# Gathers paced by the phase of the routing, experts looked up by two ranks, weighted one-hots on two engines

## The chip, the core and the metric

One core of a Trainium2 chip runs the whole program. The metric is the device time of one execution in microseconds, over three runs: median 3159.07 us (3156.07 to 3160.61). Engines are named as in the profile: PE (matrix products), DVE (vector), ACT (activations), POOL (GpSimd, which issues the gathers), SP (which issues most plain DMAs).

## The reference, cut to what matters

The program is two transformer blocks over 512 tokens of width 1024, in float32. The change is inside the feed-forward part of the first, a product-key mixture of 16384 experts with eight heads and 16 experts a head and token:

```python
def peer_ffn(h, wq, sub_keys, u, v):
    tok = h.reshape(-1, PEER_BLOCK, D)               # blocks of 128 tokens
    def block(t):
        q = (t @ wq).reshape(PEER_BLOCK, PEER_HEADS, 2, PEER_DQ // 2)
        s = jnp.einsum('tpcd,pckd->tpck', q, sub_keys)
        s1, i1 = lax.top_k(s[:, :, 0], PEER_TOPK)    # 16 of 128 first keys
        s2, i2 = lax.top_k(s[:, :, 1], PEER_TOPK)    # 16 of 128 second keys
        cand = (s1[..., :, None] + s2[..., None, :]).reshape(PEER_BLOCK, PEER_HEADS, 256)
        cidx = (i1[..., :, None] * PEER_NKEYS + i2[..., None, :]).reshape(PEER_BLOCK, PEER_HEADS, 256)
        top, pos = lax.top_k(cand, PEER_TOPK)
        idx = jnp.take_along_axis(cidx, pos, axis=-1)
        g = jax.nn.softmax(top, axis=-1)
        a = jax.nn.gelu(jnp.einsum('tpkd,td->tpk', u[idx], t), approximate=False)
        return jnp.einsum('tpk,tpkd->td', g * a, v[idx])
    return lax.map(block, tok)
```

## The kernel before, in words

The expert part does the same thing in two ways. For block 0 of the tokens it fetches the rows of U and V of each chosen expert. For blocks 1 to 3 it computes all experts densely: expert number e = 128 a + b, and a *hidden layer* (`hidden`, called 128 times, "an expert" in what follows is one such call) multiplies 128 rows of U with the 384 tokens of the three blocks and applies Gelu; a gate matrix W, zero where nothing was chosen, weights the result; the *products* multiply it with 128 rows of V.

**The routing** (`route`, L1199) goes through five phases t. In phase t below 4 `topk` (L1236) finds the experts of block t, on DVE: 16 scans of 128 scores (`top16`, L1228: two `max`, two `max_index` and one `match_replace` each), then 50 candidate sums and their 50 expert numbers, then a scan of the candidates of each head, which gives the place of each of 16 winners among the 50. The number is looked up by comparing the place with 0 to 49 (`eq`, L1271), multiplying by the candidates' numbers (L1273) and summing (L1274). Exp and a sum make the gates. In phases 2 to 4 `spread` (L1296) turns block t - 1 into the gate matrix: for each group of four tokens DVE compares 0 to 127 with the first half of the expert numbers (`oh`, L1313) and with the second (`go`), ACT scales each `go` by its gate (L1317), PE multiplies them for each token (L1329), ACT copies the result to W (L1330), and each sixteen tokens W goes to HBM (`Wd`).

**The hidden layers** run at the same time (`ahead`, L1353): 512 KB of U are loaded, split into two float32r parts by ACT (L1341) and DVE (`wl`, L1342), PE does 24 products of 384 columns, ACT the Gelu (L1350), and the activations are stored (`Ad`). 112 of them are woven with the routing, 4 follow, and the last 12 are computed among the products.

**The gathers** (`gathered`, L1123) serve block 0. POOL issues an indirect DMA of 128 rows (L1135) into one of five buffers `gr`; three loads later DVE multiplies (L1154 for U, with a sum; L1159 for V, added to `accg`). There are 256. Each DVE multiply is queued behind the DVE instruction that was last written as `self.anchor`. Gathers that the routing has not issued (`gather_left`) are spread over the first 120 of the product steps (L1062).

**The products** (`operands`, L1359; `products`, L1378): for each expert the activations (`act`), every eighth time a block of gates (`Wr`, 1.5 MB) and 512 KB of V are loaded from the SP queue; DVE multiplies activation and gate (L1371), both are split in two, and PE does 18 products of 512 columns.

**What sets the order.** `weave` (L65) runs three generators by a virtual time that each counts up by what it yields: the routing (`topk` and `spread`, run side by side by `merge`), the hidden layers (`PACE` each) and the gathers (`GATHER` for two loads). The one that is furthest behind writes its next piece. PE runs exactly in the order written. The other engines' queues are ordered by a planner from the order written and from the times that it expects, so that DVE may do a later block's top-k early, but the queue is fixed when the program starts.

## Time and profile before

| | before |
|---|---|
| median of 3 runs | 3159.07 us (3156.07 to 3160.61) |
| the profiled execution | 3161.74 us, span 3159.9 us |
| PE busy | 2967.1 us (94%) |
| DVE busy | 1900.2 us (60%) |
| ACT busy | 1268.5 us (40%) |
| POOL busy | 472.1 us (15%) |

The page divides the span into 40 slices of 79 us. In a row of it each digit is the busy share in tenths. Times below are from the start of the span. In a row of groups the mean duration of one instruction stands after the busy time; behind the bar is the idle time of the engine ahead of these instructions and what ended it. Instructions that follow each other on DVE or ACT overlap a little, so that durations add up to more than the time that passes. A busy PE is modelled: an idle time on it is idle, a busy time need not be at its peak.

### The profile page before, as it was taken

To read this page: it belongs to the slowest core of one execution; us is meant where nothing else is said; L and a number is where in the kernel's file an instruction comes from. 1 tells how busy PE (TensorE), PEld (TensorE's weight loads), DVE (VectorE), ACT (ScalarE), POOL (GpSimd) and SP (SyncE) were. 2 spreads that over 40 slices of the span, in tenths; PEclk is the share of its full clock that TensorE was granted. 3 is DMA by queue.
4 is the path that set the end of the run, shared out by engine and by line. 5 is a ranking of instruction groups with operands and counts; after the bars stand their busy time and mean duration, and the time that the engine had idled before them with its cause. 6 is when DMAs were issued, how large, how long until landed. Compare 5 with 4: busy or idle time off the path is not lost.

```text
span 3159.9 us, 42417 instructions
## 1 busy us (share of the span) xinstructions
PE 2967.1 (94%) x16073; PEld 2540.5 (80%) x16073; DVE 1900.2 (60%) x3614; ACT 1268.5 (40%) x2275; POOL 472.1 (15%) x464
## 2 busy tenths in 40 slices
PE   7999889999999999898898888899999999999998
PEld 5887787799899999777776767778888887788887
DVE  5744487539999856588788885544333235533323
ACT  4233464343376677532223323432433234433222
POOL 2101332000111111043344441000000000000000
PEclk9999899999999999999999999999999999999999
DMA  6622202235766766799999996223333322133332
GB/s 245 230 61 75 62 1 71 97 114 162 233 218 235 252 229 234 270 356 365 356 348 349 365 360 225 67 74 97 94 96 94 100 87 68 48 92 95 94 106 80
DMA packets 257165, 537.79 MB, mean 170 GB/s; under 512 B 20160, under 2 KB 135104, under 8 KB 252608
## 3 DMA queue, kind: packets, MB, share of 16 engines
q1 hardware_dynamic: 196512, 345.82, 33.9%
q0 software_dynamic: 36864, 134.23, 12.1%
q10 hardware_dynamic: 23584, 55.03, 4.6%
q8 instruction: 126, 2.06, 0.3%
q14 instruction: 79, 0.65, 0.1%
HBM read 484.93 MB, written 50.08 MB: 169 GB/s over the span
## 4 chain that ended last, share of the span: by engine, by line
PE 58%; DVE 18%; DMA 8%; issue 3%; ACT 1%; POOL 1%; SPq 0%; DVEq 0%; ACTq 0%; POOLq 0%
PE bank L122 56%; DMA act<-Ad 6%; DVE wl L1342 2%; DVE accg L1159 2%; DVE gr L1154 2%; DVE vl L135 2%; DVE sl L135 1%; DVE act L1371 1%; PE bank L606 1%; PE bank L1470 1%; DVE idx L1274 1%; DVE tmp L1232 1%; DVE eq L1271 1%; DVE eq L1273 1%; DVE go L1313 1%
## 5 line engine op out<-in xcount | busy, mean ns | idle before, releaser
L122 PE MATMUL bank<-hh,wl 128*128 128x512 f32 (+2 forms) x2304 | 839.2, 365 | 45.9 <-DVE wl L1342 32.2
L122 PE MATMUL bank<-hh,wh 128*128 128x512 f32 (+2 forms) x2304 | 843.6, 367 | 15.1 <-ACT wh L1341 5.3
L122 PE MATMUL bank<-hl,wh 128*128 128x512 f32 (+2 forms) x2304 | 833.0, 362 | 1.1 <-DVE hl L272 0.6
L149 DVE TENSOR_TENSOR wl<-w,wh 128x1024 fp32r<-128x1024 f32 (+2 forms) x280 | 303.4, 1084 | 651.5 <-ACT wh L148 643.8
L148 ACT ACTIVATE wh<-w 128x1024 fp32r<-128x1024 f32 (+2 forms) x280 | 257.4, 920 | 751.7 <-PE bank L122 609.9
L122 PEld LDWEIGHTS bank<-hh,wl 128*128 128x128 f32 x2304 | 438.4, 190 | 106.0 <-DVE wl L1342 42.6
L122 PEld LDWEIGHTS bank<-hh,wh 128*128 128x128 f32 x2304 | 438.0, 190 | 66.7 <-ACT wh L1341 6.1
L122 PEld LDWEIGHTS bank<-hl,wh 128*128 128x128 f32 x2304 | 438.6, 190 | 50.5 <-DVE hl L530 1.4
L122 PE MATMUL bank<-vh,sh 128*128 128x512 f32 x768 | 249.6, 407 | 43.6 <-ACT sh L133 24.5
L1135 POOL DMA_INDIRECT gr<-in_Un_dram,iu x128 | 165.9, 1296 | 738.7 <-DVE accg L1159 496.6
L122 PE MATMUL bank<-vl,sh 128*128 128x512 f32 x768 | 251.6, 410 | 19.2 <-DVE vl L135 19.0
L122 PE MATMUL bank<-vh,sl 128*128 128x512 f32 x768 | 247.1, 404 | 0.0
L133 ACT ACTIVATE sh<-act 128x384 fp32r<-128x384 f32 x128 | 67.1, 525 | 383.0 <-DVE act L1371 346.5
L122 PEld LDWEIGHTS bank<-vh,sh 128*128 128x128 f32 x768 | 150.5, 198 | 79.3 <-ACT sh L133 27.4
L1342 DVE TENSOR_TENSOR wl<-w,wh 128x1024 fp32r<-128x1024 f32 x128 | 155.8, 1219 | 77.4 <-ACT wh L1341 77.4
L1341 ACT ACTIVATE wh<-w 128x1024 fp32r<-128x1024 f32 x128 | 134.9, 1055 | 165.1 <-PE bank L122 142.3
L122 PEld LDWEIGHTS bank<-vl,sh 128*128 128x128 f32 x768 | 150.7, 199 | 58.6 <-DVE vl L135 27.3
L122 PEld LDWEIGHTS bank<-vh,sl 128*128 128x128 f32 x768 | 151.3, 197 | 33.5 <-DVE sl L135 0.3
L1135 POOL DMA_INDIRECT gr<-in_V_dram,iv x128 | 150.2, 1174 | 175.7 <-DVE gr L1154 107.3
L216 POOL TENSOR_TENSOR r<-r,mhalf 128x1 f32<-128x1 f32 x37 | 21.8, 591 | 1026.5 <-DVE r L215 1019.8
L135 DVE TENSOR_TENSOR vl<-w,vh 128x1024 fp32r<-128x1024 f32 x128 | 156.3, 1221 | 12.7 <-ACT vh L133 12.3
L1159 DVE SCALAR_TENSOR_TENSOR accg<-gr,wt,accg 128x1024 f32<-128x1024 f32 x127 | 162.4, 1279 | 0.0
(375 smaller groups left out, 4889.8 us busy)
## 6 DMA issues: line engine op xcount, KB each, us to landing
w<-in_U_dram SPq DMA_DIRECT2D x128, 512.0 KB, 4.6
w<-in_V_dram SPq DMA_DIRECT2D x128, 512.0 KB, 7.1
w<-in_wgu_dram SPq DMA_DIRECT2D x84, 512.0 KB, 3.7
Wd<-W ACTq DMA_DIRECT2D x24, 1024.0 KB, 6.7
Wr<-Wd SPq DMA_DIRECT2D x16, 1536.0 KB, 17.9
w<-in_wdown_dram SPq DMA_DIRECT2D x44, 512.0 KB, 3.6
Ad<-act ACTq DMA_DIRECT2D x116, 192.0 KB, 3.8
act<-Ad SPq DMA_DIRECT2D x116, 192.0 KB, 6.8
```

The lines of the kernel that those rows point to most:

```text
L122: return self.nc.tensor.matmul(out, a, b, start=start, stop=stop)
L133: self.nc.scalar.activation(hi, src, AF.Copy)
L135: (low or self.nc.vector).tensor_tensor(out=lo, in0=src, in1=hi, op=OP.subtract)
L148: self.nc.scalar.activation(hi[:, :, :n], w[:, :, :n], AF.Copy)
L149: (self.low or self.nc.vector).tensor_tensor(out=lo[:, :, :n], in0=w[:, :, :n], in1=hi[:, :, :n], op=OP.subtract)
L606: nc.tensor.matmul(o, x[k], y[:, kk, :256], start=k == 0 and i == 0 and t % 2 == 0, stop=k == KC - 1 and i == 2, skip_group_check=True)
L1135: nc.gpsimd.indirect_dma_start(out=t, out_offset=None, in_=table, in_offset=bass.IndirectOffsetOnAxis(ap=idx, axis=0))
L1154: nc.vector.scalar_tensor_tensor(t, t, 1.0, self.h0, op0=OP.mult, op1=OP.mult, accum_out=dots[:, h, k:k + 1])
L1159: nc.vector.scalar_tensor_tensor(acc, t, wt[:, h, k:k + 1], acc, op0=OP.mult, op1=OP.add)
L1232: nc.vector.match_replace(tmp, val[:, 0:8], src, -3e38)
L1341: nc.scalar.activation(uh, w, AF.Copy)
L1342: nc.vector.tensor_tensor(out=ul, in0=w, in1=uh, op=OP.subtract)
```

## The change

Three things are changed, and one constant that goes with them.

- *Gathers.* `GATHER`, the virtual time of two loads, was 11.0 throughout and is now a number for each phase of the routing: 14, 14, 11, 4.3, 1.7.
- *Lookup.* The candidates are laid out as 16 + 7 x 8 + 8 = 80 sums in place of 50, in three additions, and no numbers are formed for them. From the place of a winner a new function, `ranks`, computes its rank in the first list and its rank in the second; each is compared with 0 to 15, multiplied by that list's 16 numbers and summed, for four heads at once. Both halves of the expert number come out at once.
- *Weighted one-hots.* Of the four `go` of a group, the second and fourth are made by one DVE instruction (equal, times the gate), the first and third by two on ACT: the square of (0 to 127 less the number), then Relu of (gate - gate x square). The numbers and gates are also kept negated.
- `PACE` goes from 2.95 to 2.65; the virtual times that `topk` yields are changed as well.

```diff
--- before.py
+++ after.py
@@ -23,14 +23,14 @@
 TD = S - T0
 AHEAD = 116
 REST = 4
-PACE = 2.95
+PACE = 2.65
 GROUP = 8
 WBUFS = 4
 LAG = 1
 WT = 16
 GBUFS = 5
 GAHEAD = 3
-GATHER = 11.0
+GATHER = (14.0, 14.0, 11.0, 4.3, 1.7)
 OPS_LAG = 2
 TAIL = 2
 STATE = 3.0
@@ -1161,7 +1161,7 @@
                     nc.scalar.activation(wt[:, h], dots[:, h], AF.Gelu)
                     nc.vector.tensor_tensor(out=wt[:, h], in0=wt[:, h], in1=g[:, h], op=OP.mult)
             if n % 2:
-                yield GATHER
+                yield GATHER[self.phase]
 
     def queries(self, mv, first):
 
@@ -1203,6 +1203,7 @@
         self.routing = True
         cur = None
         for t in range(5):
+            self.phase = t
             gens = []
             if t < 4:
                 gens.append(self.topk(pq, sc[t], io))
@@ -1244,45 +1245,33 @@
                 yield 1.0
         f1 = pq.tile([128, 8, 2, 16], F32, name="f1")
         nc.vector.tensor_copy(f1, i1)
-        nc.vector.tensor_scalar(f1[:, :, 0], f1[:, :, 0], 128.0, None, op0=OP.mult)
-        cand = pq.tile([128, 8, 50], F32, name="cand")
-        cidx = pq.tile([128, 8, 50], F32, name="cidx")
-        for dst, src in ((cand, m1), (cidx, f1)):
-            o = 0
-            for a in range(8):
-                n = 16 // (a + 1)
-                nc.vector.tensor_tensor(out=dst[:, :, o:o + n], in0=src[:, :, 0, a:a + 1].to_broadcast([128, 8, n]),
-                                        in1=src[:, :, 1, :n], op=OP.add)
-                o += n
-            nc.vector.tensor_tensor(out=dst[:, :, o:], in0=src[:, :, 0, 8:],
-                                    in1=src[:, :, 1, 0:1].to_broadcast([128, 8, 8]), op=OP.add)
-        yield 2.7
+        cand = pq.tile([128, 8, 80], F32, name="cand")
+        nc.vector.tensor_tensor(out=cand[:, :, :16], in0=m1[:, :, 0, 0:1].to_broadcast([128, 8, 16]), in1=m1[:, :, 1], op=OP.add)
+        nc.vector.tensor_tensor(out=cand[:, :, 16:72].rearrange("p h (a b) -> p h a b", a=7),
+                                in0=m1[:, :, 0, 1:8].unsqueeze(3).to_broadcast([128, 8, 7, 8]),
+                                in1=m1[:, :, 1, None, :8].to_broadcast([128, 8, 7, 8]), op=OP.add)
+        nc.vector.tensor_tensor(out=cand[:, :, 72:], in0=m1[:, :, 0, 8:],
+                                in1=m1[:, :, 1, 0:1].to_broadcast([128, 8, 8]), op=OP.add)
+        yield 1.2
         top = pq.tile([128, 8, 16], F32, name="top")
         pos = pq.tile([128, 8, 16], U32, name="pos")
         for h in range(8):
             tmp = pq.tile([128, 128], F32, name="tmp", bufs=2)
-            self.top16(top[:, h], pos[:, h], cand[:, h], tmp[:, :50])
-            yield 0.6
-        pf = pq.tile([128, 8, 16], F32, name="pf")
-        nc.vector.tensor_copy(pf, pos)
-        idx = pq.tile([128, 128], F32, name="idx", bufs=2)
-        for h in range(8):
-            eq = pq.tile([128, 16, 50], F32, name="eq")
-            nc.vector.tensor_tensor(out=eq, in0=io[:, None, :50].to_broadcast([128, 16, 50]),
-                                    in1=pf[:, h].unsqueeze(2).to_broadcast([128, 16, 50]), op=OP.is_equal)
-            self.anchor = nc.vector.tensor_tensor(out=eq, in0=eq, in1=cidx[:, h:h + 1].to_broadcast([128, 16, 50]), op=OP.mult)
-            nc.vector.tensor_reduce(idx[:, h * 16:(h + 1) * 16], eq, axis=AX.X, op=OP.add)
-            yield 2.7
-        ii = pq.tile([128, 128], I32, name="ii")
-        nc.vector.tensor_copy(ii, idx)
-        e1 = pq.tile([128, 128], F32, name="e1", bufs=2)
-        e2 = pq.tile([128, 128], F32, name="e2", bufs=2)
-        it = pq.tile([128, 128], I32, name="it", bufs=2)
-        nc.vector.tensor_scalar(it, ii, 7, None, op0=OP.logical_shift_right)
-        nc.vector.tensor_copy(e1, it)
-        it = pq.tile([128, 128], I32, name="it", bufs=2)
-        nc.vector.tensor_scalar(it, ii, 127, None, op0=OP.bitwise_and)
-        nc.vector.tensor_copy(e2, it)
+            self.top16(top[:, h], pos[:, h], cand[:, h], tmp[:, :80])
+            yield 0.7
+        ab = self.ranks(pq, pos, cand)
+        E = pq.tile([128, 2, 8, 16], F32, name="E", bufs=2)
+        for h in range(0, 8, 4):
+            hs = slice(h, h + 4)
+            for c in range(2):
+                eq = pq.tile([128, 4, 16, 16], F32, name="eq")
+                nc.vector.tensor_tensor(out=eq, in0=io[:, None, None, :16].to_broadcast([128, 4, 16, 16]),
+                                        in1=ab[c][:, hs].unsqueeze(3).to_broadcast([128, 4, 16, 16]), op=OP.is_equal)
+                self.anchor = nc.vector.tensor_tensor(out=eq, in0=eq, op=OP.mult,
+                                                      in1=f1[:, hs, c].unsqueeze(2).to_broadcast([128, 4, 16, 16]))
+                nc.vector.tensor_reduce(E[:, c, hs], eq, axis=AX.X, op=OP.add)
+                yield 3.4
+        e1, e2 = (E[:, c].rearrange("p h k -> p (h k)") for c in range(2))
         g = pq.tile([128, 8, 16], F32, name="g", bufs=2)
         nc.vector.tensor_tensor(out=g, in0=top, in1=top[:, :, 0:1].to_broadcast([128, 8, 16]), op=OP.subtract)
         nc.scalar.activation(g, g, AF.Exp)
@@ -1293,28 +1282,50 @@
         yield 2.5
         return e1, e2, g.rearrange("p h k -> p (h k)")
 
+    def ranks(self, pq, pos, room):
+
+        nc = self.nc
+        row, low, a, t = (room[:, :, i * 16:i * 16 + 16] for i in range(4))
+        for x, s, op in ((row, 3, OP.logical_shift_right), (low, 7, OP.bitwise_and)):
+            i = pq.tile([128, 8, 16], U32, name="ri")
+            nc.vector.tensor_scalar(i, pos, s, None, op0=op)
+            nc.vector.tensor_copy(x, i)
+        nc.vector.scalar_tensor_tensor(t, row, 9.0, low, op0=OP.is_ge, op1=OP.mult)
+        nc.vector.tensor_scalar(a, row, -1.0, 0.0, op0=OP.add, op1=OP.max)
+        nc.vector.tensor_tensor(out=a, in0=a, in1=t, op=OP.add)
+        nc.vector.tensor_tensor(out=low, in0=low, in1=t, op=OP.subtract)
+        nc.vector.tensor_scalar(row, row, 1.0, 8.0, op0=OP.is_equal, op1=OP.mult)
+        nc.vector.tensor_tensor(out=row, in0=row, in1=low, op=OP.add)
+        return a, row
+
     def spread(self, pq, t, e1, e2, g, io):
 
         nc = self.nc
         b = self.bank()
         for i, x in enumerate((e1, e2, g)):
             nc.tensor.transpose(b[:, i * 128:(i + 1) * 128], x, self.ident)
-        eT = pq.tile([128, 2, 128], F32, name="eT", bufs=2)
-        nc.vector.tensor_copy(eT, b[:, :256].rearrange("p (a t) -> p a t", a=2))
-        gT = pq.tile([128, 128], F32, name="gT", bufs=2)
-        nc.vector.tensor_copy(gT, b[:, 256:384])
+        eT = pq.tile([128, 128], F32, name="eT", bufs=2)
+        nc.vector.tensor_copy(eT, b[:, :128])
+        gT = pq.tile([128, 2, 2, 128], F32, name="gT", bufs=2)
+        eg = b[:, 128:384].rearrange("p (a t) -> p a t", a=2)
+        nc.vector.tensor_copy(gT[:, 0], eg)
+        nc.vector.tensor_scalar(gT[:, 1], eg, -1.0, None, op0=OP.mult)
         todo = []
         for q in range(128 // WT):
             W = pq.tile([128, 128, WT], F32, name="W", bufs=2)
             for r in range(WT // 4):
                 c = q * WT + r * 4
                 oh, go = (pq.tile([128, 4, 128], F32, name=n, bufs=LAG + 2) for n in ("oh", "go"))
-                for i, o in enumerate((oh, go)):
-                    self.anchor = nc.vector.tensor_tensor(
-                        out=o, in0=io.unsqueeze(1).to_broadcast([128, 4, 128]),
-                        in1=eT[:, i, c:c + 4].unsqueeze(2).to_broadcast([128, 4, 128]), op=OP.is_equal)
+                self.anchor = nc.vector.tensor_tensor(
+                    out=oh, in0=io.unsqueeze(1).to_broadcast([128, 4, 128]),
+                    in1=eT[:, c:c + 4].unsqueeze(2).to_broadcast([128, 4, 128]), op=OP.is_equal)
                 for i in range(4):
-                    nc.scalar.activation(go[:, i], go[:, i], AF.Copy, scale=gT[:, c + i:c + i + 1])
+                    e, w, ne, nw = (gT[:, s, a, c + i:c + i + 1] for s in range(2) for a in range(2))
+                    if i % 2:
+                        self.anchor = nc.vector.tensor_scalar(go[:, i], io, e, w, op0=OP.is_equal, op1=OP.mult)
+                    else:
+                        nc.scalar.activation(go[:, i], io, AF.Square, bias=ne)
+                        nc.scalar.activation(go[:, i], go[:, i], AF.Relu, bias=w, scale=nw)
                 todo.append((q, r, W, oh, go))
                 if len(todo) > LAG:
                     self.spread_mm(t, *todo.pop(0))
```

## Rows read from the trace of the kernel before

**Rows 1.** First line of the page: span and instructions.
```profile
span 3159.9 us, 42417 instructions
```

**Rows 2.** Windows: stretch, its length, busy us (instructions) by engine, clock, DMA share, GB/s.
```profile
715.00:865.00 150.00, 139.69 (x785) 134.53 (x784) 150.00 (x543) 54.35 (x77) 18.40 (x14) 1.00 0.62 201
865.00:1040.00 175.00, 167.09 (x1032) 165.50 (x1031) 173.79 (x566) 120.40 (x232) 19.98 (x15) 0.98 0.67 223
1040.00:1201.00 161.00, 158.59 (x1002) 157.53 (x1001) 113.58 (x147) 113.66 (x222) 25.09 (x18) 1.00 0.74 249
1201.00:1309.00 108.00, 102.89 (x644) 97.58 (x643) 66.25 (x90) 87.04 (x190) 10.47 (x8) 1.00 0.63 225
1309.00:1334.00 25.00, 13.70 (x77) 13.11 (x75) 13.65 (x18) 9.16 (x13) 2.96 (x3) 0.82 0.95 333
1334.00:1897.00 563.00, 499.69 (x2031) 401.15 (x2032) 459.57 (x632) 165.40 (x227) 227.20 (x191) 0.92 1.01 357
```

**Rows 3.** The page's part 6: issues, KB each, median us from issue to landing.
```profile
w<-in_V_dram SPq DMA_DIRECT2D x128, 512.0 KB, 7.1
...
Wr<-Wd SPq DMA_DIRECT2D x16, 1536.0 KB, 17.9
...
act<-Ad SPq DMA_DIRECT2D x116, 192.0 KB, 6.8
```

**Rows 4.** Instructions on the gathered rows (tile gr): ns min/median/max, and landings in us.
```profile
L1135 POOL DMA_INDIRECT gr<-in_Un_dram,iu x128: 939/1014/2149, 781.2 to 1874.7; - x128
...
L1159 DVE SCALAR_TENSOR_TENSOR accg<-gr,wt,accg x127: 1270/1279/1286, 987.7 to 2017.8; 128x1024 f32<-128x1024 f32 x127
...
DMA to landing us min/median/max: 4.1/7.3/10.2
```

**Rows 5.** Chain of waits, 2200 to 2600 us: start us, us, what.
```profile
2231.40 355.90 PE bank L122 x1582
```

**Rows 6.** Timeline of DVE, 744 to 747 us: start us, us, what.
```profile
744.54 0.98 DVE L1271 TENSOR_TENSOR eq<-io,pf 128x800 f32<-128x800 f32 x1
745.44 1.22 DVE L1342 TENSOR_TENSOR wl<-w,wh 128x1024 fp32r<-128x1024 f32 x1
```

**Rows 7.** Groups by line and shape, DVE, 705 to 1312 us: busy us, mean ns | idle before.
```profile
L1342 DVE TENSOR_TENSOR wl<-w,wh 128x1024 fp32r<-128x1024 f32 x113 | 137.5, 1218 | 49.8 <-ACT wh L1341 49.8
L1313 DVE TENSOR_TENSOR oh<-io,eT 128x512 f32<-128x512 f32 x96 | 65.8, 685 | 38.8 <-PE bank L122 38.6
...
L1154 DVE SCALAR_TENSOR_TENSOR gr<-gr,h 128x1024 f32<-128x1024 f32 x33 | 39.9, 1218 | 2.5 <-DMA gr<-in_Un_dram,iu 2.5
L1271 DVE TENSOR_TENSOR eq<-io,pf 128x800 f32<-128x800 f32 x32 | 31.5, 985 | 0.1
...
L1230 DVE MAX8 m<-sc 128x8 f32<-128x128 f32 x64 | 17.9, 282 | 11.8 <-PE bank L122 11.8
...
L1230 DVE MAX8 top<-cand 128x8 f32<-128x50 f32 x32 | 6.1, 202 | 0.0
```

**Rows 8.** Groups by line and shape, DVE, whole span.
```profile
L529 DVE TENSOR_SCALAR h<-raw,a,m 128x512 f32<-128x512 f32 x8 | 4.3, 545 | 0.3
```

**Rows 9.** Groups by line and shape, ACT, 1201 to 1309 us.
```profile
L1350 ACT ACTIVATE act<-bank 128x384 f32<-128x384 f32 x16 | 7.7, 482 | 17.5 <-PE bank L122 17.5
```

**Rows 10.** Groups by line and shape, ACT, whole span.
```profile
L1317 ACT ACTIVATE go<-go,gT 128x128 f32<-128x128 f32 x384 | 123.9, 392 | 40.0 <-DVE go L1313 37.7 <-ACT act L1350 0.4
...
L148 ACT ACTIVATE wh<-w 128x512 fp32r<-128x512 f32 x80 | 50.4, 632 | 107.4 <-PE bank L122 61.2 <-PE bank L606 30.5 <-issue 8.1
...
L1350 ACT ACT_TABLE_LOAD x5 | 6.4, 1283 | 0.1
L528 ACT ACTIVATE hh<-raw,m,a 128x512 fp32r<-128x512 f32 x8 | 6.4, 811 | 3.8 <-DVE a L526 3.7
```

## The prediction

> **What bounds the kernel now.** I took the profiled execution as a whole first: its span is 3159.9 us [rows 1] and its time 3161.7 us, 2.7 us above the median of 3159.07 us. Differences are worked out in its own times and taken off the median at the end. Then I cut its middle into stretches and read the busy time of every engine in each [rows 2]. The cuts stand where the Gelu of experts 0, 33, 65, 96 and 112 begins, which is about where the routing passes from block to block. The reader is to see three things there. From 715 to 1040 us DVE is busy all the time (150.00 of 150.00 us, 173.79 of 175.00) and PE is idle for 18 us in all. From 1040 to 1309 us PE is nearly full (158.59 of 161, 102.89 of 108) while DVE has 47 and 42 us free. From 1334 to 1897 us, where the products run, the DMA share is 1.01 at 357 GB/s, and PE, DVE and POOL all have time left. So the routing is bound by DVE first and by PE afterwards, and the product stretch by DMA bandwidth.
>
> Third view: what the product stretch moves [rows 3]. PE has 2031 matmuls there, 18 an expert, so 113 experts. Each costs 512 KB of V, 192 KB of stored activations and an eighth of 1536 KB of gates: 0.918 MB. A gather brings 128 rows of 1024 floats [rows 4], 0.524 MB, and POOL issues 191 of them in the stretch [rows 2]. 113 x 0.918 + 191 x 0.524 = 204 MB; 563 us at 357 GB/s are 201 MB. The account closes, and half of the bytes are gathers. The change is about those.
>
> **How many gathers move.** The routing, the hidden layers and the gathers are woven by the numbers that they yield, so the counts follow from the source. Before, a block's top-k yields 47.6 and a spread 46.4, the five phases together 329.6; an expert costs 2.95, so 112 experts end with the routing. A pair of gathers costs 11, and phases 1 to 4, in which they run, yield 282: 26 pairs. After, a top-k yields 38.9, the phases together 294.8, an expert costs 2.65: again 112, as 15, 15, 32, 32 and 18 in the phases (before 17, 16, 32, 31, 16). Followed step by step, the gathers become 3, 8, 19 and 26 pairs in phases 1 to 4 (before 5, 8, 9, 4): 56 pairs in place of 26. The 73 left over (before 103) are spread over the product stretch. 60 gathers, 31.5 MB, leave it; 44 of them go into the last phase of the routing, 20 into the one before, and phase 1 has 4 fewer.
>
> **Term 1, the product stretch.** Bandwidth alone gives 31.5 MB / 357 GB/s = 88 us. But PE has a floor: a long run of matmuls of the same 512 columns takes 355.90 us for 1582 [rows 5], 0.225 us each, so 2034 take 458 us, against (201 - 31.5) / 357 = 475 us for the bytes. With two limits 17 us apart and gates that come in bursts of 1536 KB, landing 17.9 us after issue [rows 3], they will not overlap perfectly. I take 495 us, 68 us less than 563. The bounds are 88 less, and 48 less (515 us) if the bursts cost as many gaps as now.
>
> **Term 2, DVE in the routing.** In the dense part DVE starts an instruction some 0.08 us before the one ahead ends (eq takes 0.98 us and the next starts 0.90 after it) [rows 6], so I charge durations less 0.08. Top-k, per block: 24 passes over 800 elements (three like eq [rows 7] for each head) become 12 over 1024, priced as wl at 1.218 [rows 7]: 24 x 0.90 - 12 x 1.14 = 8.0 us saved. The 18 additions that make candidates and their numbers (0.12 each, as a scan of 50 elements) become 3 over 640 elements together: 1 us saved. The 40 scans of candidates go from 50 to 80 elements; between 202 ns at 50 and 282 at 128 [rows 7] that is 31 ns each: 1.2 us more. Taking the place apart into two ranks is ten small instructions for seven, three more of 128 elements at 0.2: 0.6 more. Four blocks: 29 us saved. Spread, per group of four tokens: one compare of 512 (like oh, 685 ns [rows 7], 0.60 dense) becomes two instructions over 128 elements with two column operands. No such row exists. The nearest is the same instruction over 512, 545 ns [rows 8]; at the rate of half a cycle an element that is 0.345 for 128, and at a full cycle 0.41: 0.53 to 0.66 us a pair. 96 groups: between 7 us saved and 6 lost; nearer to the row, I take 5 saved. Gathers add 60 x 1.2 us [rows 4, 7] = 72. DVE was busy 504 us from 715 to 1309 [rows 2] and would be 504 - 34 + 72 = 542, of a stretch that PE fills for 568. In sum it fits; the place decides.
>
> **Term 3, phases 0 to 3** (486 us before, for 96 experts). Two experts move into the last phase: -10 us at 5.1 us each. DVE saves 29 + 3 here and gets 16 gathers more, 19 us; since it was the limit up to 1040 us, PE's 18 us of idle time there shrink. I take 8 back. Below this lies the whole 18; above it nothing, should phase 3, which now has 38 gathers, lose what the first ones win. Sum -18 us.
>
> **Term 4, the last phase** (1201 to 1309 us, 16 experts [rows 9]). DMA moved 225 GB/s there [rows 2]: 24.3 MB, 4.2 of them gathers. With 18 experts the rest becomes 22.6, and 52 gathers add 27.3: 49.9 MB. At 357 GB/s that is 140 us. DVE would need 52 x 1.2 + 18 x 1.14 + 32 x 1.15 = 120 us, PE its 103 us and two experts more at under 4.5 (150 us for 33 of them up to 865), about 112. So DMA becomes the bound, where it stood at 0.63. I take 144 us, 36 more than 108. Bounds: 128 (+20, if the five buffers and the loads ahead carry some of it over the edges) and 170 (+62, if the waits for landings show on PE as well).
>
> ACT: four instructions a group as before, but the nearest rows to the new ones differ. One column operand at 128 elements takes 392 ns; two column operands at 512 take 811, against 632 without any [rows 10], so 0.09 for each. Square is then 0.39 and Relu 0.48, and Relu reads what Square wrote. That is 0.2 to 0.4 us more a group, 20 to 40 us over 96 groups, on an engine that is idle for 21 us of the last phase and for 47 to 96 us of the earlier stretches [rows 2]. I cost it at nothing. Should it come onto the path in the last phase it is 32 x 0.4 = 13 us. In return ACT no longer waits for DVE's second compare.
>
> One rule of the Trainium skill speaks against moving these one-hots to DVE: "SBUF — State Buffer", section "Who interferes with whom", says that a tensor_scalar in a two-port mode holds a port pair that GpSimd needs to write the descriptors of its DMAs, and that the later one waits. No run here shows it. By that rule the last phase would have 64 such instructions of 0.26 us in POOL's way, at most 17 us, and 3109 would become 3126 at most.
>
> **Sum.** -68 - 18 + 36 = -50 us: 3159.07 - 50 = 3109 us.
>
> **Rivals.**
> A. As summed, 3109 us (3085 to 3135): 52%.
> B. Only the bytes count: the last phase is stretched to 128 us, the products fall to 475. -88 - 18 + 20 = -86: 3073 us. For it: the account of bytes closes. Against it: the 17 us between the two limits. 20%.
> C. The products are held by the bursts and by PE: -48 - 18 + 36 = -30: 3129 us. 13%.
> D. Slower: DVE's one queue. The multiply of a gather stands ahead of the next expert's wl; when it waits for its rows, PE waits too. If each pair of gathers costs a full landing, 7.3 us [rows 4], and one multiply, the last phase takes 52 x 4.25 = 221 us, 113 more: 113 - 18 - 68 = +27, 3186 us. It decides from 194 us on for that phase, 3.7 us a gather. For it: landings up to 10.2 us under full load. Against it: in the routing DVE has waited 2.5 us in all for a gather [rows 7], five buffers hold more than one pair, and the products now take a gather each 2.9 us (563 / 191). 10%.
> E. The table of ACT: should Relu not lie in the set that Gelu uses, every expert of phases 2 to 4 needs two loads of 1283 ns [rows 10], 82 x 2.57 = 210 us on ACT: some 3300 us. Relu has no row before. The Trainium skill, "ScalarE: Activation LUTs", section "Table sets: the hidden batching unit", counts relu among the functions of every set; by it the case is out. 2%.
> The remaining 3%: the places where gathers land cancel the gain, no change.
>
> **Range and chances.** From B with a little room, 3062, to a last phase at its upper bound with C's products (-48 - 18 + 62 = -4: 3155), 3160. Where A holds, 3085 to 3135. This kernel's measurements can tell about 0.2%, 6 us, from no change. A, B and C are all faster by more: 85%, less 1 for C with that last phase, so 84%. D and E are slower: 12%. Within 0.2% stays 4%.
>
> **What would show it.** In the trace after: 52 gathers between the Gelu of expert 94 and that of expert 112, with the DMA share near 1 and 135 to 150 us long (term 4). Some 131 gathers in the product stretch, 485 to 505 us long, PE busy for over nine tenths of it (term 1). The three passes of the lookup 16 in number for four blocks each, 1.2 us each (term 2). The first 94 experts within 460 to 475 us, with less idle time on PE before 1040 us (term 3). No table load at Square or Relu. The forecast is wrong if the product stretch still takes over 530 us, or if the routing grows by more than it gives back.

## The result, and the profile after

The changed kernel takes 3246.47 us (median of 4 runs, 3240.85 to 3251.76) beside 3159.84 us for the kernel before on the same chip: a ratio of 1.0272, 95% interval 1.0256 to 1.0289. It is slower by 87 us where the prediction said 50 us faster. The stretches of the profiled execution, cut like [rows 2] at the Gelu of experts 0, 30, 62, 94 and 112 and at the products:

```profile
span 3243.0 us, 42564 instructions
```

```profile
710.00:844.00 134.00, 128.35 (x722) 123.25 (x720) 134.00 (x517) 51.31 (x75) 17.16 (x12) 1.00 0.61 204
844.00:1020.00 176.00, 164.43 (x1017) 162.27 (x1018) 165.21 (x542) 122.64 (x227) 16.98 (x12) 0.99 0.64 213
1020.00:1203.00 183.00, 170.34 (x1029) 168.42 (x1028) 120.27 (x191) 118.66 (x225) 59.03 (x38) 0.95 0.80 282
1203.00:1351.00 148.00, 118.16 (x692) 114.01 (x691) 116.50 (x188) 97.05 (x194) 90.78 (x52) 0.90 0.91 325
1351.00:1376.00 25.00, 12.62 (x72) 11.98 (x70) 12.50 (x16) 9.40 (x14) 2.01 (x2) 0.82 0.92 319
1376.00:1990.00 614.00, 511.15 (x2021) 402.90 (x2022) 395.38 (x542) 162.40 (x225) 164.55 (x135) 0.93 0.85 283
```

The gathers went where they were expected: 38 and 52 in the last two phases, 135 in place of 191 in the product stretch (some 131 were expected). But that stretch, with 29 MB less to move, grew from 563 to 614 us, and its DMA share fell from 1.01 to 0.85. Measured exactly, from the first multiply of activation and gate to the one of expert 112, the products went from 568.2 to 618.6 us. The parts of the span add up: 5 us less ahead of the routing, phases 0 to 3 +7 (485.9 us for 96 experts to 493.1 for 94), last phase +40 (107.7 for 16 to 147.6 for 18), between routing and products +3, products +50, what follows them -12: +83 us, as the spans say (3159.9 to 3243.0).

What was late in the products stands in the waits of that stretch (who waited for whom: us in all, times, longest), here before the change,

```profile
DVE act L1371 <- DMA act<-Ad: 101.5, 16, 8.9
...
PE bank L122 <- DVE vl L135: 19.0, 11, 6.1
```

and after it (PEld is PE's load of weights):

```profile
DVE act L1382 <- DMA act<-Ad: 215.4, 76, 8.1
PEld bank L122 <- DVE vl L135: 121.9, 51, 6.5
PE bank L122 <- DVE vl L135: 100.5, 47, 6.1
```

DVE's multiply of activation and gate waits for the load of the activations 76 times, 215 us in all, and PE then waits 100 us for `vl`, the part of V that DVE splits off. The transfers themselves had become quicker, as the issues of the stretch show (KB each, median us to landing; [rows 3] has 7.1, 17.9 and 6.8):

```profile
w<-in_V_dram SPq DMA_DIRECT2D x108, 512.0 KB, 5.6
Wr<-Wd SPq DMA_DIRECT2D x15, 1536.0 KB, 10.3
act<-Ad SPq DMA_DIRECT2D x109, 192.0 KB, 5.3
```

One such wait in the timelines of SP, DVE and PE (start, us, what, and idle time ahead with what ended it):

```profile
1506.74 0.33 SPq L1378 DMA_DIRECT2D act<-Ad  x1
```

```profile
1506.16 0.56 DVE L135 TENSOR_TENSOR sl<-act,sh 128x384 fp32r<-128x384 f32 x1
1507.80 0.56 DVE L1382 TENSOR_TENSOR act<-act,Wr 128x384 f32<-128x384 f32 x1 [1.08 <-DMA act<-Ad]
1508.27 1.22 DVE L135 TENSOR_TENSOR vl<-w,vh 128x1024 fp32r<-128x1024 f32 x1
1509.41 0.17 DVE L1162 TENSOR_TENSOR wt<-wt,gw 128x16 f32<-128x16 f32 x1
1513.86 0.56 DVE L1382 TENSOR_TENSOR act<-act,Wr 128x384 f32<-128x384 f32 x1 [4.29 <-DMA act<-Ad]
1514.34 1.28 DVE L1159 SCALAR_TENSOR_TENSOR accg<-gr,wt,accg 128x1024 f32<-128x1024 f32 x1
1515.54 0.55 DVE L135 TENSOR_TENSOR sl<-act,sh 128x384 fp32r<-128x384 f32 x1
1516.00 1.22 DVE L135 TENSOR_TENSOR vl<-w,vh 128x1024 fp32r<-128x1024 f32 x1
```

```profile
1512.85 0.62 PE L122 MATMUL bank<-vh,sl 128*128 128x512 f32 x2
...
1517.28 1.20 PE L122 MATMUL bank<-vl,sh 128*128 128x512 f32 x2 [3.36 <-DVE vl L135]
1518.28 1.05 PE L122 MATMUL bank<-vh,sl 128*128 128x512 f32 x2
```

`sl` at 1506.16 reads an activation tile for the last time and frees one of the three buffers; SP issues the next load into it at 1506.74; the multiply that needs that load stands on DVE almost directly behind, and DVE stops until 1513.86. `vl` of an earlier expert stands behind that multiply, at 1516.00, and PE runs dry at 1517.28. After its idle time a pair of matmuls takes 1.05 us where it took 0.62: the granted clock, 1.00 up to there, has fallen to 0.50, the lower of its two levels (1.2 of 2.4 GHz):

```profile
1510.00:1517.00 7.00, 3.92 (x18) 2.89 (x16) 3.14 (x4) 1.48 (x3) 1.01 (x1) 1.00 0.51 195
...
1518.00:1520.00 2.00, 2.00 (x7) 1.52 (x6) 1.86 (x5) 0.77 (x2) 1.24 (x1) 0.50 0.92 298
```

The order is written into DVE's queue. Counted in the traces, the multiply of expert e stands right ahead of the `vl` of the same expert in 105 of 128 places in the kernel before, and ahead of that of e - 1 in 9. After the change it stands ahead of the `vl` of e - 2 in 80 places and of e - 1 in 31. (The expectations below count two more each time, "two" and "three" before, "three or four" after, "five or six" with more buffers; two `vl` run before the first multiply.) The products of e - 2 are written right after the loads and splits of e (`OPS_LAG`), so the `vl` of e - 2 is one that PE needs next. With three buffers, the load for expert e cannot be issued before `sl` of e - 3. In the kernel before, the `sl` of e - 2 and of e - 1 both stand between that one and the multiply of e in 118 places; after the change neither does in 63, and only one in 48.

The smaller prices came out near their rows. Busy time, mean ns and idle time ahead of ACT's and DVE's new instructions, 710 to 1351 us:

```profile
L1328 ACT ACTIVATE go<-go,gT 128x128 f32<-128x128 f32 x192 | 86.6, 485 | 1.2 <-ACT go L1327 0.5
L1327 ACT ACTIVATE go<-io,gT 128x128 f32<-128x128 f32 x192 | 68.1, 394 | 3.7 <-DVE gT L1312 3.4
```

```profile
L1325 DVE TENSOR_SCALAR go<-io,gT 128x128 f32<-128x128 f32 x192 | 57.6, 345 | 0.0
L1268 DVE TENSOR_TENSOR eq<-io,cand 128x1024 f32<-128x1024 f32 x16 | 19.6, 1223 | 0.0
L1272 DVE TENSOR_REDUCE E<-eq 128x64 f32<-128x1024 f32 x16 | 19.4, 1215 | 0.0
```

There is no table load at Square or Relu: the loads stand at the same places and in the same number, 18, as before.

### The profile page after: what moved, and what is told of

Its sections match the earlier page's. It is cut to its first block, busy times and chain, and to the rows that moved or that the text cites. A ratio compares the mean times of both kernels' runs of the same rounds, so it can differ in the third digit from the quotient of the medians.

```text
span 3243.0 us, 42564 instructions
## 1 busy us (share of the span) xinstructions
PE 2988.2 (92%) x16073; PEld 2554.3 (79%) x16073; DVE 1867.1 (58%) x3617; ACT 1279.2 (39%) x2275; POOL 515.1 (16%) x464
## 4 chain that ended last, share of the span: by engine, by line
PE 39%; DMA 11%; DVE 8%; issue 2%; SPq 0%; ACT 0%; POOL 0%; DVEq 0%; POOLq 0%; ACTq 0%
PE bank L122 38%; DMA act<-Ad 10%; DVE accg L1159 2%; DVE vl L135 1%; DVE sl L135 1%; DVE gr L1154 1%; PE bank L1481 1%; SPq L1378 0%; DVE act L1382 0%; DMA gr<-in_Un_dram,iu 0%; DMA Ad<-act 0%; PE bank L266 0%; DVE hl L272 0%; POOL r L216 0%; DMA sk<-in_sinks_dram 0%
## 5 line engine op out<-in xcount | busy, mean ns | idle before, releaser
L122 PE MATMUL bank<-vl,sh 128*128 128x512 f32 x768 | 260.3, 422 | 101.5 <-DVE vl L135 101.5
L1135 POOL DMA_INDIRECT gr<-in_Un_dram,iu x128 | 185.0, 1445 | 772.9 <-DVE accg L1159 473.6
L1135 POOL DMA_INDIRECT gr<-in_V_dram,iv x128 | 179.0, 1399 | 179.3 <-DVE accg L1159 83.7
L1382 DVE TENSOR_TENSOR act<-act,Wr 128x384 f32<-128x384 f32 x128 | 71.0, 558 | 225.8 <-DMA act<-Ad 225.4
L1154 DVE SCALAR_TENSOR_TENSOR gr<-gr,h 128x1024 f32<-128x1024 f32 x128 | 156.1, 1221 | 33.4 <-DMA gr<-in_Un_dram,iu 33.4
```

The costliest lines, as they stand in the source:

```text
L122: return self.nc.tensor.matmul(out, a, b, start=start, stop=stop)
L1135: nc.gpsimd.indirect_dma_start(out=t, out_offset=None, in_=table, in_offset=bass.IndirectOffsetOnAxis(ap=idx, axis=0))
L1154: nc.vector.scalar_tensor_tensor(t, t, 1.0, self.h0, op0=OP.mult, op1=OP.mult, accum_out=dots[:, h, k:k + 1])
L1382: self.anchor = nc.vector.tensor_tensor(out=a3, in0=a3, in1=self.Wr[:, :, e % GROUP], op=OP.mult)
```

## The experiments

All ratios are to the kernel before on the same chip; "routing" is from the Gelu of expert 0 to that of expert 112, "products" as defined above, all three in the profiled execution.

| kernel | median us | ratio (95%) | routing | last phase | products |
|---|---|---|---|---|---|
| before | 3159.07 | | 593.6 | 107.7 | 568.2 |
| after | 3246.47 | 1.0272 (1.0256 to 1.0289) | 640.7 | 147.6 | 618.6 |
| anchored | 3136.73 | 0.992 (0.9894 to 0.9946) | 634.6 | 145.7 | 513.6 |
| act5 | 3223.75 | 1.02 (1.0176 to 1.0224) | 639.3 | 145.6 | 595.8 |
| paced | 3230.87 | 1.0218 (1.0191 to 1.0244) | 630.8 | 124.3 | 611.8 |
| flat | 3180.66 | 1.0077 (1.005 to 1.0104) | 615.6 | 131.5 | 564.5 |
| lookup | 3163.43 | 1.002 (1.0007 to 1.0032) | 599.4 | 116.8 | 571.2 |
| onehots | 3185.39 | 1.0087 (1.0068 to 1.0106) | 623.4 | 131.4 | 567.0 |
| before_anchored | 3145.43 | 0.9966 (0.9955 to 0.9977) | 592.8 | 107.7 | 563.0 |
| lookup_anchored | 3128.81 | 0.991 (0.9894 to 0.9927) | 623.2 | 131.2 | 511.0 |
| held | 3188.68 | 1.0096 (1.0079 to 1.0113) | 623.0 | 131.0 | 566.6 |
| all_dve | 3141.18 | 0.9946 (0.9929 to 0.9962) | 578.9 | 94.5 | 565.8 |
| paced_anchored | 3129.05 | 0.9899 (0.988 to 0.9918) | 625.8 | 125.8 | 510.9 |
| early | 3113.73 | 0.9862 (0.9844 to 0.9881) | 638.2 | 138.0 | 483.8 |
| wh_ahead | 3156.99 | 0.9995 (0.998 to 1.0009) | 594.5 | 110.4 | 571.4 |
| before_wh_ahead | 3148.42 | 0.9972 (0.9956 to 0.9989) | 584.3 | 100.6 | 564.1 |
| early_dve | 3109.35 | 0.9855 (0.9825 to 0.9885) | 630.6 | 140.8 | 482.3 |
| early_dve_2 | 3109.4 | 0.9849 (0.9832 to 0.9865) | 630.5 | 142.6 | 485.4 |
| early_dve_oldlookup | 3128.17 | 0.9908 (0.9891 to 0.9924) | 646.8 | 134.6 | 491.4 |

The last phase holds 18 experts in the kernels with the new yields of the top-k and a pace of 2.65 (after, anchored, act5, flat, lookup, lookup_anchored, early, early_dve, early_dve_2) and 16 in the others.

**The products: DVE's queue.** *anchored* puts the multiply behind the last `vl` written:

```diff
-        self.anchor = nc.vector.tensor_tensor(out=a3, in0=a3, in1=self.Wr[:, :, e % GROUP], op=OP.mult)
+        with self.after(self.last_vl) if e else ExitStack():
+            self.anchor = nc.vector.tensor_tensor(out=a3, in0=a3, in1=self.Wr[:, :, e % GROUP], op=OP.mult)
```

> The changed kernel with one edge more: in the products the multiply of activations by gates (A) is queued on DVE behind the low part of V (vl) of the expert before. Theory 1, DVE's queue: since the change A stands three or four experts ahead of vl, directly behind the multiply that frees its buffer, so DVE stops for each landing and vl and PE wait behind it. Then the product stretch (614 us between 1376 and 1990) falls to 490 to 515 us, DVE's waits for activations from 215 us to under 60, and the time from 3246 to about 3130 us. Rival, too few buffers: the loads are issued late whatever the order, the order only moves the wait; 3220 to 3246 us. Rival, traffic: the gathers left over land badly among V and gates; no difference, 3246.

The products fall by 105 us, to 513.6, and the whole by 110, below the kernel before, as theory 1 had it. The queue now has the multiply right ahead of its own `vl` in 113 places. The waits that were 215.4 and 100.5 us:

```profile
DVE act L1383 <- DMA act<-Ad: 58.0, 14, 7.4
...
PE bank L122 <- DVE vl L135: 9.8, 9, 1.6
```

and the stretch itself, where the DMA share is 0.97 and PE busy for 482.88 of 510 us:

```profile
1372.00:1882.00 510.00, 482.88 (x2040) 391.60 (x2041) 398.61 (x544) 163.95 (x225) 193.03 (x135) 0.96 0.97 337
```

*act5* gives the activations more buffers:

```diff
-            a = pm.tile([128, TD], F32, name="act", bufs=3)
+            a = pm.tile([128, TD], F32, name="act", bufs=5)
```

> The changed kernel with five buffers for the activations of the product steps in place of three, order left to the planner. Its DVE queue has A five or six experts ahead of vl, again directly behind what frees the buffer. Theory 1: each A still waits for a full landing with vl queued behind it, 3220 to 3260 us. Rival, too few buffers: loads are issued two experts earlier and the waits go, 3120 to 3150 us.

Only 23 us come back. With five buffers the multiply moves still further forward in DVE's queue, ahead of the `vl` of e - 3 (56 places) or of e - 4 (46), and waits as before (195.5 us in all, PE 93.2 for `vl`), as theory 1 said. Buffers don't cure an order that uses them up.

*paced* is the kernel before with the new pacing alone, *flat* the kernel after without it:

```diff
 # paced: kernel before
-GATHER = 11.0
+GATHER = (15.4, 15.4, 12.1, 4.7, 1.8)
 # flat: kernel after
-GATHER = (14.0, 14.0, 11.0, 4.3, 1.7)
+GATHER = (9.9, 9.9, 9.9, 9.9, 9.9)
```

> The kernel before with the gathers' price by phase alone (15.4, 15.4, 12.1, 4.7, 1.8 in its own virtual times, 56 pairs in the routing); lookup, one-hots and pace of the hidden layers as before. Theory 1: the whole loss is in the pacing; products 605 to 625 us, last phase 30 to 45 us longer; 3240 to 3270 us. Rival, the lookup or the one-hots cost the time: under 3150 us.

> The changed kernel with the same price for a pair of gathers in all phases, 9.9, so that 26 pairs run in the routing as before the change; lookup by ranks and the one-hots on two engines stay. Its DVE queue in the products is that of the kernel before. Theory 1: the product stretch is 555 to 570 us as before, the routing some 10 us shorter than before; 3140 to 3155 us. Rival, the lookup or the one-hots cost the time: 3200 us or more.

The pacing alone makes the long products (611.8) and DVE's queue of the kernel after; without it both are as before (564.5). So it is the pacing that moves the multiply, through the planner; why the planner draws it forward when fewer gathers' multiplies stand in that stretch no run shows. Both runs missed their times. paced, expected at 3240 us or more with a last phase 30 to 45 us longer, took 3230.87 with 17 us more; flat, expected at 3140 to 3155 with a shorter routing, took 3180.66, its routing 22 us longer. So theory 1 holds for the products and not for the whole loss: something in the routing costs time without the pacing. *before_anchored* and *paced_anchored* are the kernel before with the edge alone, and with edge and pacing:

> The kernel before with the multiply of activations by gates queued behind vl of the expert before, as in the changed kernel with that edge. Its DVE queue has A two experts ahead of vl in 105 places of 128 already and three ahead in 9, so little moves: theory 1 says products of 560 to 568 us and 3150 to 3160 us. If the edge helped by itself, whatever the gathers, it would show here: under 3140.

> The kernel before with the new pacing alone and the edge that puts the multiply of the gates behind the subtraction vl of the expert before; lookup and one-hots as before. Theory (the queue of DVE took the gain of the pacing): products 508-520 us as in anchored (pacing alone: 612), routing 622-632 (pacing alone: 631), the median 3159 - 54 + 33 = 3138, between 3128 and 3145. Rival (the edge works only together with the shorter lookup, which frees DVE): products over 540 us, the median 3160 or more.

The edge alone is worth 0.3% (3145.43 us, between the two expectations). With it the pacing is worth the 57 us in the products that it should have given from the start, 568.2 to 510.9, and the kernel is 1.0% faster without any other part of the change.

**The routing: one part at a time.** *lookup* has the new lookup alone (and the pace of 2.65 with 9.9 for a pair of gathers, which is the old proportion); *onehots* the new `spread` alone in the kernel before; *lookup_anchored* is the kernel after with the old `spread` and the edge.

```diff
 # onehots: kernel before, with spread of the change, and
+        gT = pq.tile([128, 2, 2, 128], F32, name="gT", bufs=1)
 # lookup: kernel after, with spread of the kernel before, and
+GATHER = (9.9, 9.9, 9.9, 9.9, 9.9)
```

> The changed kernel with the one-hots of before (compare on DVE, scale on ACT) and a flat price of 9.9 for the gathers: of the change only the lookup by two ranks and the pace of 2.65 are left. With a flat price and both parts the time was 3180.7 us, the routing 615.6 us against 593.6 before, its last phase with PE waiting for ACT's wh. Theory A, the one-hots put 0.2 to 0.4 us a group on ACT in front of wh: then this kernel has a routing of 580 to 592 us and takes 3140 to 3158 us. Rival B, the lookup or the pace does it: routing over 605 us, 3170 us or more.

> The kernel before with the weighted one-hots half on ACT and half on DVE, and nothing else of the change (one buffer in place of two for the transposed gates, for room). Theory A: ACT is late with wh in phases 2 and 4; routing 608 to 620 us, 3175 to 3190 us. Rival B: the one-hots are free, 3150 to 3162 us.

> Lookup by ranks, gathers by phase as in the change, one-hots of before, and the multiply by gates queued behind vl. With the new one-hots and the edge: 3136.7 us, routing 634.6, products 513.6. Theory A gives back 10 to 25 us of the routing: 3112 to 3128 us. Rival B: no difference, 3130 to 3140.

The lookup alone gives nothing: its 3163.43 us and its routing of 599.4 lie between the two expectations, and 0.2% above the kernel before. The one-hots cost 30 us of routing, 24 of them in the last phase. Of the waits there, three lines stand out (in the kernel before the first two are 5.0 and 0.2 us, and the third is not there):

```profile
DVE wl L1348 <- ACT wh L1347: 36.7, 15, 5.1
...
PE bank L122 <- ACT wh L1347: 10.5, 4, 3.3
PE bank L122 <- ACT go L1323: 6.8, 8, 0.9
```

ACT was busy for 92.78 of those 131 us. Two experiments asked whether it is ACT at all, and whether its order:

```diff
 # held: Square waits for the group's compare on DVE
+                        with self.after(first):
+                            nc.scalar.activation(go[:, i], io, AF.Square, bias=ne)
 # all_dve: no go on ACT
+                    self.anchor = nc.vector.tensor_scalar(go[:, i], io, e, w, op0=OP.is_equal, op1=OP.mult)
```

> The new one-hots alone in the kernel before, as in the experiment onehots, and one edge more: ACT's Square and Relu of a group wait for DVE's compare of the same group, as the scaled copies of the kernel before do. ACT's work is the same. Theory (ACT's order: the new instructions wait for nothing, run ahead, and the copy wh of the next hidden layer stands behind them): the last phase of the routing falls from 131 to 108-117 us, DVE's wait for wh from 37 to under 15 us, the median to 3158-3170. Rival (ACT's load, or DVE's two more small instructions): the last phase stays at 127-133 us and the median at 3180-3190.

> The new one-hots alone in the kernel before, but all four tokens of a group made on DVE by the compare-and-multiply instruction (0.34 us measured), none on ACT. ACT is freed of 1.75 us a group, DVE gets 2 x 0.26 = 0.5 us a group more, 17 us in the last phase. Theory (ACT is the place): the last phase 108-120 us in place of 131, DVE's wait for wh near the 5 us of before, the median 3155-3172. Rival (DVE's instructions are what the last phase lost): the last phase at 140 us or more, the median 3195 or more.

*all_dve* takes the last phase to 94.5 us, under the 107.7 of the kernel before and the 108 to 120 expected: ACT is the place, and DVE had the room. *held* measured nothing new: its edge was met already, and ACT's queue came out word for word as in onehots. Its 131.0 us fit the rival's number without speaking for it. ACT's queue over two experts of the last phase, in the order of the traces (G Gelu, c scaled copy, s Square, r Relu, W copy to W, H `wh`; onehots goes to and fro between the two patterns beside the `|`):

```
before            GccccWccccWccccccccHGWWH
onehots, held     GsrsWrssrrWssrrssrrHGWWs | GrsWrssrrWHssrrssrrHHGWWs
wh_ahead          HGsrsWrssrrWHssrrssrGrWW
before_wh_ahead   HGccccWccccWHccccccGcWcW
```

In the kernel before a `wh` stands right behind the last two W. In onehots it comes one pattern later, behind eight instructions on `go`, a Gelu and two more W, which wait for PE; then there are three. *wh_ahead* writes load, `wh` and `wl` of each expert one expert earlier, *before_wh_ahead* does the same in the kernel before:

```diff
-        uh = self.st.tile([128, 2, 512], FR, name="wh")
...
+        uh, ul = self.held_u.pop(e, None) or self.split_u(e)
+        if e + 1 < AHEAD:
+            self.held_u[e + 1] = self.split_u(e + 1)
```

> The new one-hots alone in the kernel before, as in onehots, with load, wh and wl of each expert's U written one expert earlier in the program. ACT's instructions are the same, but its queue in the last phase now has one wh per expert, behind two copies of W, where onehots has one and then three, the late ones behind 8 to 12 Square and Relu. Theory (the order of ACT's queue): the last phase 106-118 us in place of 131, DVE's wait for wh under 15 us, the median 3155-3170. Rival (ACT's time per group: the Relu that reads what Square wrote): the last phase 126-133 us, the median 3178-3190.

> Control: the kernel before with the same earlier writing of load, wh and wl and nothing else. Both theories: the last phase 105-110 us and the median 3154-3164, since its queue had one wh per expert already. Over 1% faster would say that the earlier writing helps by itself, and the difference between wh_ahead and this run is then what the one-hots cost.

With the same instructions in another order the last phase falls from 131 to 110.4 us. The control is at 100.6, below the 105 to 110 expected, so the earlier writing helps by itself, by 7 us. If it is worth as much beside the one-hots, 14 of the 24 us that these cost were order; the 10 that are left have a wait of their own, Relu ending late for PE, which the control doesn't show. DVE's wait for `wh` was expected under 15 us and is 21.2, but the control has 19.4 of it:

```profile
DVE wl L1349 <- ACT wh L1348: 21.2, 16, 3.4
...
PE bank L122 <- ACT go L1323: 10.9, 16, 0.8
```

**What the findings give.** *early* is lookup_anchored with more gathers in phases 2 and 3; *early_dve* the kernel after with the edge, that pacing and all `go` on DVE; *early_dve_oldlookup* the same with the lookup of before and yields scaled to suit.

```diff
-GATHER = (14.0, 14.0, 11.0, 4.3, 1.7)
+GATHER = (14.0, 14.0, 8.0, 3.0, 1.7)
```

> The best version so far (new lookup, new pacing, old one-hots, the edge; 3128.8) with more gathers in phases 2 and 3, in which the DMA share was 0.64 and 0.80: yields of 8 and 3 in place of 11 and 4.3, some 10 pairs more, 10.5 MB. Theory (bytes and PE's floor bound the products once the queue is mended): products 485-495 us in place of 511, routing 628-640 in place of 623, the median 3108-3124. Rival (the multiplies that wait for landings stretch phases 2 and 3 by as much, 3 us a pair): products fall by the same 20 us and the routing grows by 25 or more, the median 3130-3145.

> The kernel after with the edge behind vl, the pacing of early (8 and 3 in phases 2 and 3) and all four one-hots of a group on DVE. Theory (ACT was the place of the one-hots' cost, the queue of DVE that of the products): routing 612-628 us (early, with the old one-hots: 638), products 482-488, the median 3092-3108. Rival (DVE, full in phases 0 to 2 and with multiplies that wait for landings, has no room for 2 x 96 instructions more): routing 636-650, the median 3112-3128.

> early_dve once more, on the chip of the next run, to be compared with it: 3105-3115 as it gave 3109 before.

> early_dve with the lookup by one place among 50 of the kernel before, and the yields of experts and gathers scaled by 2.95/2.65, so that about as many gathers fall into each phase. The new lookup saves some 29 us of DVE's busy time in four blocks. If DVE holds the routing now: 3120-3140. If it does not (as the single change, 1.002, would have it): 3098-3115.

*early* leaves 112 gathers in the products, which take 483.8 us; PE is busy for 465.77 of 488.80 there. It gives 27 us in the products for 15 in the routing. *early_dve*, twice at 3109 us, has the lowest median, 1.5% below the kernel before, but its ratio is not clear of early's. Its routing, 630.6, lies between the two expectations: with this many gathers in the last phase, taking the one-hots from ACT no longer shortens it (140.8 after 138.0). DVE is nearly full there and PE waits 24.7 us for `wl`:

```profile
1198.00:1338.00 140.00, 114.77 (x678) 111.09 (x678) 132.45 (x250) 55.52 (x69) 72.24 (x54) 0.91 0.96 352
```

```profile
PE bank L122 <- DVE wl L1349: 24.7, 11, 4.3
```

The lookup that gave nothing alone is worth 19 us here (3109.4 against 3128.17; 16 of them in the routing, 630.5 against 646.8, the rest in the products, which hold 112 and 118 gathers).

## Why the prediction was wrong

**The failed step is term 1.** It took bytes and PE as the only limits of the product stretch: "Bandwidth alone gives 31.5 MB / 357 GB/s = 88 us. But PE has a floor". The bytes did go. With the order mended the pacing alone gives 57 us (568.2 to 510.9) and anchored 55, within the bounds of 48 to 88 but less than the 68 taken, and DMA and PE are both near their limits there. What failed is that DVE's order would stay. A planner writes that queue from the work it is given, and taking gathers' multiplies away was costed as if the rest kept its place. The trace of before had the line that should have warned: 101.5 us of DVE waiting for `act`. Little of it reached PE, which waited 19.0 us for `vl`, as the `vl` behind that multiply was one that PE needed only two experts later. The error of this step is 118 us (+50 for -68), of 137 in all.

**ACT "at nothing" failed as well.** The durations were right (0.394 and 0.485 us for 0.39 and 0.48), so was the added load, but the reason given, idle time on ACT, says nothing on where `wh` stands. It cost 24 us in the last phase as a single change, above the 13 allowed. The promised return, that ACT no longer waits for DVE's compare, gave nothing that shows. It is tempting to say that losing this wait let the new instructions run ahead of `wh`, but held puts a wait for DVE back and has the same queue, so why the planner put them there stays open. In the kernel after, the one-hots cost less: lookup_anchored, here first, against anchored, 11 us of routing and 14.5 of the last phase.

```profile
1208.10:1339.30 131.20, 113.52 (x689) 109.62 (x688) 117.30 (x157) 93.03 (x193) 69.63 (x52) 0.95 0.98 368
```

```profile
1202.60:1348.30 145.70, 116.25 (x690) 111.98 (x689) 116.07 (x187) 96.87 (x193) 89.61 (x52) 0.91 0.92 333
```

Not all of these 14.5 us need be ACT: POOL's 52 instructions, the issues of the gathers, take 89.61 us there in place of 69.63, and no run parts the two.

**Term 4** came out at +40 for +36, with 52 gathers as counted, and is near for two reasons of which one was not in it. With the old one-hots the mechanism holds: lookup_anchored, with the same 18 experts and 52 gathers, is at its DMA limit (0.98) and takes 131.2 us, at 368 GB/s where 357 were assumed. That is +24, of which the gathers alone make 17 (paced, 124.3 with 16 experts). The other 16 us are the one-hots, costed at nothing: in the kernel after DMA stood at 0.91, PE was idle for 30 of 148 us and had a granted clock of 0.90. That both add up to nearly +36 is luck.

**Term 3** was -18 and is +7. Phases 0 to 2 took 14 us less with three experts less, 5.0 us an expert as before, so the time that DVE saved did not show; phase 3 took 183.0 us for 32 experts where 161.4 were needed for 31. That is the gathers, 38 there: paced alone, with 34, has 179.5 for 31 experts, flat, with the old number, 163.5 for 32. The upper bound, nothing gained "should phase 3 lose what the first ones win", was the nearer one.

**Term 2** was right in its durations (passes of 1.2 us, 16 each in four blocks; DVE's pair at 0.345 each) and gave nothing as a single change (1.002); DVE is busy there for 475 us of the routing in place of 504, so the 29 us were saved, and why the routing is no shorter stays open. With both queues mended it gives 19 us.

**The rivals.** D had the right mechanism, DVE's one queue with PE's operand behind a wait for a landing, at the wrong place: it was priced for gathers in the routing, and came with activations in the products. In the last phase the gathers made DVE wait for 15 us in all. B's products, 88 us shorter (480 as they are measured here), were not reached even with 112 gathers in them (482.3 to 485.4). E is out. On the two-port rule of the Trainium skill ("SBUF — State Buffer", "Who interferes with whom"), 17 us at most by the prediction, the runs do not decide. POOL's instructions did grow in the last phase of the kernel after, 52 of them to 90.78 us (1.75 each) from lookup_anchored's 69.63 (1.34). But early_dve, with twice as many of DVE's compare-and-multiply instructions in that phase, has 72.24 us for 54 (1.34 each). So the growth does not go with the number of those instructions, POOL's durations are rough, and what makes it stays open.

## What to carry to other kernels

Where a planner fixes an engine's queue, taking work from that engine can reorder what stays: compare the queues of both kernels and ask of every instruction that waits for a transfer what stands behind it, and how far ahead of its turn it stands. A load's reader that stands just behind the instruction that frees its buffer waits for most of a landing each time; here an edge that put it behind the operand that PE needs cured it, and more buffers did not. Idle time on an engine is no cover for added work unless the order leaves the instruction that others wait for in its place.

## What the runs showed of the hardware

In the last phase of onehots the granted clock falls after idle times of PE, and the slower matmuls cost more than the added idle time itself. In one place PE is busy for 2.37 of 5 us and then runs 19 matmuls in a full 5 us at a mean clock of 0.57, most of the time at the lower of its two levels:

```profile
1254.00:1259.00 5.00, 2.37 (x8) 1.75 (x7) 2.43 (x4) 5.00 (x12) 0.00 (x0) 0.75 0.19 53
1259.00:1264.00 5.00, 5.00 (x19) 5.00 (x18) 1.23 (x1) 1.09 (x2) 0.00 (x0) 0.57 0.57 195
1264.00:1274.00 10.00, 9.02 (x62) 8.64 (x61) 6.19 (x12) 7.09 (x14) 0.06 (x1) 1.00 0.55 203
```

The same 639 matmuls of that phase keep PE busy for 110.94 us there, at a mean clock of 0.91, and, without such stops, for 99.06 in wh_ahead, whose clock is 1.00; onehots first:

```profile
1204.00:1335.00 131.00, 110.94 (x639) 104.39 (x638) 63.68 (x121) 92.78 (x189) 10.44 (x8) 0.91 0.53 187
```

```profile
1194.00:1304.00 110.00, 99.06 (x639) 96.01 (x638) 63.82 (x119) 93.19 (x189) 11.43 (x8) 1.00 0.65 222
```

Of the 21 us between the two, 12 are longer matmuls and 9 idle time; 9% of 131 us, what the clock lacked, are 12 us too.
